# A hybrid layer's norms: reciprocal square roots by a power on GpSimd in place of Newton steps on VectorE

## The chip, the cores and the metric

The kernel runs on one core of a Trainium2 chip. The metric is the device time of one launch, in microseconds (us). The engines are named as in the profile: PE is TensorE (PEld its weight loads), DVE is VectorE, ACT is ScalarE, POOL is GpSimd, and SP is the engine that issues the transfers.

## The reference

One layer over a sequence of 2048 tokens of width 1024, all in float32. The rows of x are normalized and projected to the inputs of three mixers: a gated delta rule (4 heads of 128), an mLSTM (4 heads of 64) and an S5 state-space mixer (256 channels). Their outputs are projected back and added to x. A feed-forward with a convolution over tokens (2816 channels) and a last norm of the rows follow. Cut to the lines that matter here:

```python
def rms_norm(x, w):                      # rows, three times
    return x * lax.rsqrt(jnp.mean(x * x, -1, keepdims=True) + EPS) * w
def head_rms_norm(x, w):                 # outputs of the delta rule and the mLSTM
    return x * lax.rsqrt(jnp.mean(x * x, -1, keepdims=True) + EPS) * w
def l2_norm(x):                          # q and k of the delta rule
    return x * lax.rsqrt(jnp.sum(x * x, -1, keepdims=True) + EPS)

h = rms_norm(x, norm1_w);  proj = h @ w_in
q = l2_norm(silu(conv(q))) * GDN_DK ** -0.5;  k = l2_norm(silu(conv(k)))
y_a = head_rms_norm(gated_delta_rule_chunked(q, k, v, g, beta), norm_w) * silu(z)
y_b = sigmoid(o) * head_rms_norm(mlstm_chunked(...), norm_w)
x = x + concat(y_a, y_b, y_c) @ w_out
x = x + conv_ffn(rms_norm(x, norm2_w), ...)
return rms_norm(x, final_norm_w)
```

## The kernel before, in words

The sequence is worked through in four blocks of 512 tokens (NB = 4, BT = 512, four chunks of P = 128 tokens each). For each block a main stream of products (`main_a`) projects the normalized rows, one column tile of 128 after the other, and side streams do everything else: the delta rule of a head (`gdn`, 16 times), the mLSTM of a block (`mlstm`, four times), the S5 mixer, the preparation of the next block's rows (`x_prep`), and the rounding of weights. Then follow the output projection with the second norm (`out_proj`), the feed-forward in two halves of 1024 tokens (`ffn`), and the last norm (`final_sums`, `finals`).

Products in float32 are made of three in a shorter type: each weight tile is split into a rounded part and a rest (`split`). ACT writes the rounded part (`wh`, in the feed-forward `f_wh`), and POOL subtracts it from the tile (`wl`, `f_wl`), 1024 columns at a time. So POOL's queue holds mostly splits, and each waits for ACT.

The order in which instructions are emitted is not written out. Streams are Python generators; `drive` steps the one whose needs are met first by an estimate that the kernel itself keeps (`Clock`): it charges each instruction a cost by engine and size as it is emitted. What stands between two `yield`s of a stream is emitted in one go. Every engine then executes its instructions in the order of emission, and semaphores hold one that needs another engine's result.

The reciprocal square root is a helper, `rsqrt(y, x, t)`, on DVE alone: a guess from the bits of the float (a shift, then a multiplication and an addition of integers), and three Newton steps of three instructions. It has four callers, and each makes an affine step (scale the sum, add EPS) on DVE before it:

- `inv_rms`: norms of rows, from two half sums (tiles `rs`, `n_rs`, `f_rs`, one column for each row tile). ACT takes the squares and their sums.
- `gdn`, norms of q and k: eight columns, `s_ssq` to `s_rs`. The next instructions on DVE make `s_c` and `s_b` of the result, and from them the matrix `g_D` that POOL masks into `g_T`.
- `gdn`, the head norm: four columns, `s_so` to `s_ro`. DVE multiplies it by q's norm, scales the head's output with it into `gq`, and PE transposes that (`sd_py`).
- `mlstm`: 16 columns, all four chunks at once, after POOL has squared and DVE summed each chunk. It scales the output `mv`.

`s_t` is the temporary of the Newton steps in `gdn`. Nearly all instructions carry the line of the recording helper, L167, so groups are told apart by their tiles.

Of the kernel before, what the change touches and what calls it, by code (L numbers as in the profile page):

```python
# [7 lines left out]
F32 = mybir.dt.float32  # L8
F32R = mybir.dt.float32r
I32 = mybir.dt.int32  # L10
AF = mybir.ActivationFunctionType
ALU = mybir.AluOpType
# [3 lines left out]
DRAM = bass.MemoryType.DRAM  # L16

P = 128
L = 2048
DM = 1024  # L20
# [3 lines left out]
NCB = BT // P  # L24
# [4 lines left out]
EPS = 1e-6  # L29
# [4 lines left out]
# order of a block's heads (0-3), their gates (a-d) and the mLSTM's columns (m)  # L34
# [10 lines left out]
class Clock:  # L45
    """An estimate of when each engine reaches what was emitted for it, to order the emission by."""
# [35 lines left out]
    def span(self, ap):  # L82
        """Tile and the ranges of its elements of a partition"""
        if ap.space != SB:
            return ap.tensor.name, self.ALL
        dims = sorted((s, n) for s, n in ap.ap[1:] if n > 1 and s)
        size = 1
        while dims and (dims[0][0] <= size or len(dims) > 1 or dims[0][1] > 4):
            s, n = dims.pop(0)
            size += (n - 1) * s  # L90
        lo = ap.offset % ap.ap[0][0]
        s, n = dims[0] if dims else (0, 1)
        return ap.tensor.name, tuple((lo + i * s, lo + i * s + size) for i in range(n))

    def after(self, log, span, own, other):
        """Ends of what log has on a span: plus own[engine], or other"""
        name, rs = span
        t = 0.0
        for k, (end, by) in log.get(name, {}).items():
            if any(a < hi and lo < b for a, b in k for lo, hi in rs):  # L100
                t = max(t, end + own.get(by, other))
        return t

    def note(self, e, op, args, kw):
# [3 lines left out]
        # engines take turns at a bank  # L108
# [78 lines left out]
class Hybrid:  # L187
# [21 lines left out]
    def rsqrt(self, y, x, t):  # L209
        V = self.V  # L210
        V.tensor_scalar(out=y.bitcast(I32), in0=x.bitcast(I32), scalar1=1, scalar2=None,
                        op0=ALU.logical_shift_right)
        V.tensor_scalar(out=y.bitcast(I32), in0=y.bitcast(I32), scalar1=-1, scalar2=0x5F3759DF,
                        op0=ALU.mult, op1=ALU.add)
        for _ in range(3):
            V.tensor_tensor(out=t, in0=y, in1=y, op=ALU.mult)
            V.scalar_tensor_tensor(out=t, in0=t, scalar=-0.5, in1=x, op0=ALU.mult, op1=ALU.mult)
            V.scalar_tensor_tensor(out=y, in0=t, scalar=1.5, in1=y, op0=ALU.add, op1=ALU.mult)
# [15 lines left out]
    def setup(self):  # L234
        nc, ins, V, A, S = self.nc, self.ins, self.V, self.A, self.S
        cp = self.const = self.pool("const")
        self.dram = self.pool("dram", space=DRAM)
        self.pctx = ExitStack()
        self.ps = self.pool("ps", space=PSUM, ctx=self.pctx)
        self.ident = cp.tile([P, P], F32, name="ident")  # L240
        S.dma_start(out=self.ident, in_=self.cst_d[C_ID])

# [157 lines left out]
    def square_sums(self, xt, ss, junk):  # L400
        """ss[:, 0:2] = sums of the squares of the rows' halves"""
        for j in range(2):
            self.A.activation(out=junk, in_=xt[:, j * 512:(j + 1) * 512], func=AF.Square, accum_out=ss[:, j:j + 1])

    def inv_rms(self, out, ss, t):
        """out = 1 / rms of rows from ss (rows, n, 2)"""
        V = self.V
        V.tensor_tensor(out=t, in0=ss[:, :, 0], in1=ss[:, :, 1], op=ALU.add)
        V.tensor_scalar(out=t, in0=t, scalar1=1.0 / DM, scalar2=EPS, op0=ALU.mult, op1=ALU.add)
        self.rsqrt(out, t, ss[:, :, 0])  # L410
# [34 lines left out]
    def to_channels(self, xs, k, wcol, hi, lo, psum):  # L445
        """Channel block k of four row tiles, transposed, times the norm weight, in two parts."""
        ps = self.ps.tile([P, 4, P], F32, tag=psum[0], bufs=psum[1], name="psx")
        for j, x in enumerate(xs):
            self.T.transpose(out=ps[:, j, :], in_=x[:, k * P:(k + 1) * P], identity=self.ident)
        flat = ps.rearrange("p a b -> p (a b)")  # L450
        self.A.activation(out=hi, in_=flat, func=AF.Copy, scale=wcol)
        self.V.scalar_tensor_tensor(out=lo, in0=flat, scalar=wcol, in1=f32(hi), op0=ALU.mult, op1=ALU.subtract)

    def norm1(self, b, n, ps, w):
        """A block's normalized rows, transposed, with the products of its first column tile"""
# [23 lines left out]
    # what follows a column tile's products; tiles are followed in their order  # L479
# [72 lines left out]
    def ops_a(b):  # L552
        """Column tiles of a block: kind, index, first column of w_in."""
# [37 lines left out]
    def decay(self):  # L591
        """na = -exp(gdn_a_log)"""
# [6 lines left out]
    def gates(self, b, gs, gt):  # L599
# [18 lines left out]
        # log(1 + e) = 2 atanh(e / (2 + e))  # L618
# [9 lines left out]
        # q = log1p(e); softplus = max(y, 0) + q  # L628
        V.scalar_tensor_tensor(out=q, in0=y, scalar=0.0, in1=q, op0=ALU.max, op1=ALU.add)
        # beta = 1 / (1 + exp(y)) through e = exp(-|y|): (y < 0 ? 1 : e) / (1 + e)  # L630
# [9 lines left out]
        # g (h, c) and log f (c, h)  # L640
# [43 lines left out]
    def gdn(self, b, h, tiles, gz, gt):  # L684
        V, A, G, T, S = self.V, self.A, self.G, self.T, self.S
        n = b * H + h
# [19 lines left out]
        # transposes to token layout, with the sums of squares of k and q  # L706
# [36 lines left out]
        V.tensor_scalar(out=ssq, in0=ssq, scalar1=EPS, scalar2=None, op0=ALU.add)  # L743
        rs, t = sm("rs", 2 * NCB), sm("t", 2 * NCB)
        self.rsqrt(rs, ssq, t)
# [31 lines left out]
        # inverse of I + M by doubling of the diagonal blocks: Ti, and its transpose Vi beside it;  # L777
        # a level changes only the columns of Vi in the upper halves, those of Ti in the lower ones
# [44 lines left out]
        # the recurrence over chunks; the new values take the place of the old, the states that of the keys  # L823
# [28 lines left out]
        # head norm, gate  # L852
        so, t4 = sm("so"), sm("t4")
# [5 lines left out]
        V.tensor_scalar(out=so, in0=so, scalar1=1.0 / P, scalar2=EPS, op0=ALU.mult, op1=ALU.add)  # L859
        ro = sm("ro")  # L860
        self.rsqrt(ro, so, t4)
# [14 lines left out]
    def mlstm(self, b, kT, vT, og, gt):  # L876
# [13 lines left out]
        for c in range(NCB):  # L890
# [72 lines left out]
            # the chunk's results take the place of its values  # L963
# [8 lines left out]
        s2, s3 = tl("s2", [P, 16]), tl("s3", [P, 16])  # L972
        V.tensor_scalar(out=s1, in0=s1, scalar1=1.0 / 64, scalar2=EPS, op0=ALU.mult, op1=ALU.add)
        self.rsqrt(s2, s1, s3)
# [19 lines left out]
    def s5_setup(self, pool):  # L994
# [53 lines left out]
        # th = n pi/2 + r  # L1048
# [19 lines left out]
        # quadrant m in {-2..2}: odd: (m cos, -m sin); even: (s sin, s cos) with s = 1 - m^2 / 2  # L1068
# [58 lines left out]
        for q0 in range(0, NG, NQ):  # L1127
# [15 lines left out]
            for g0 in range(0, NQ, 4):  # L1143
# [8 lines left out]
                # the injections take the place of what was transposed  # L1152
# [9 lines left out]
        # rotor of one chunk and its modulus  # L1162
# [12 lines left out]
        # powers 0..15 of the rotor, and of its 16th power  # L1175
# [28 lines left out]
    def s5_first(self):  # L1204
        """The matrices of S5, in the place of the first block's rows"""
# [7 lines left out]
    def s5_run(self, ep, n0, N, QG):  # L1213
        """Chunks n0 .. n0 + N of the sequence, QG groups at a time; starts from self.s5c and leaves it for more."""
# [22 lines left out]
        for g0 in range(0, 16, QG):  # L1237
# [3 lines left out]
            # rotor powers 16 i + j from those of i and j  # L1241
# [15 lines left out]
            # injections, turned back  # L1257
# [82 lines left out]
    def w_out_load(self, wo, st):  # L1340
        """The two parts of w_out"""
# [20 lines left out]
    def out_prod(self, xs, y):  # L1362
        """The output projection of a tile of tokens, added to the first of xs"""
# [28 lines left out]
    def ffn_pools(self):  # L1392
        """Room for what follows the mixers, in their place"""
# [12 lines left out]
    def out_proj(self):  # L1406
        """Output projection, a tile of tokens after the other. While the last block is mixed there is room for
        the projection only, and the norm of such tiles comes later."""
# [74 lines left out]
    def norm2(self, i, x, r):  # L1483
        """A tile's rows, normalized and transposed: in two parts for the first half, to memory for the second"""
# [18 lines left out]
    class Weights:  # L1503
        """Weight tiles of the feed-forward in their order of use, loaded and split ahead."""
# [35 lines left out]
    def ffn_plan(self):  # L1540
        self.groups = [[m, m + 1] for m in range(0, MF, 2)]
        NH = L // HALF
        # the down products of a group come after the first up products of the next one
# [207 lines left out]
    def drive(self, main=None, cond=lambda: True):  # L1751
        """Steps main to its end, or without one the sides while cond holds."""
# [74 lines left out]
def _constants():  # L1827
# [8 lines left out]
    # level i: row s in the lower half of a block of 2w, column j the j-th of the columns in upper halves  # L1836
# [30 lines left out]
```

## Time and profile before

| | |
|---|---|
| time, median of 3 runs | 3026.31 us |
| the three runs | 3022.46, 3026.86, 3026.31 us |
| the profiled execution: its span, first to last instruction (the only time it is listed with) | 3025.7 us |
| PE, busy | 2798.8 us (93%) |
| DVE, busy | 2037.8 us (67%) |
| ACT, busy | 1142.8 us (38%) |
| POOL, busy | 837.1 us (28%), 536 instructions |
| mixers, until about | 1410 us |
| feed-forward, until about | 2996 us |

How to read the lines of the profile: a group's row has the engine, the operation, the tile written and the tiles read, the shapes, the count, the busy time with the mean duration in ns, and the idle time of that engine just before with what ended it. In a row of the timeline the first two numbers are the start in us from the span's start and the duration; x2 or x3 merges several alike; square brackets hold the idle time before and what ended it. A row of the waits has who waited for whom, the sum in us, how often, and the longest.

### The profile page before, as it was taken

Reading aid. Unit: us, or ns where it says so; the run is one execution under the profiler, and the core shown is the slowest. Engines: PE = TensorE matmul, PEld = TensorE weight load, DVE = VectorE, ACT = ScalarE, POOL = GpSimd, SP = SyncE. Lnnn points to the kernel's source line nnn. Section 1 sums busy time; section 2 is a strip of 40 time slices with the busy share of each in tenths; the row PEclk is TensorE's granted clock in tenths of the full one; section 3 lists DMA queues with packets and bytes.
Section 4 is the critical chain, followed back from the end, with each engine's and each line's share of the span. In section 5 each row is a group of like instructions: output and inputs, shape, how many; then the busy total and the mean of one; then the engine's idle time right before and its main releaser. Section 6 shows DMA issues by size and latency. Waiting matters only on the chain.

```text
span 3025.7 us, 37726 instructions
## 1 busy us (share of the span) xinstructions
PE 2798.8 (93%) x13826; PEld 2333.7 (77%) x13826; DVE 2037.8 (67%) x4524; ACT 1142.8 (38%) x2141; POOL 837.1 (28%) x536
## 2 busy tenths in 40 slices
PE   7887888978898888889999999999999999999997
PEld 5676777867787777678888888888888888888885
DVE  6877778688877886764446665666568665656566
ACT  4334444444454353533333333223344322333333
POOL 3253024222322342222322222222222222222223
PEclk9888899999999999979999999999999999999998
DMA  4222222223221322334561111111125111111111
GB/s 126 62 81 71 77 77 76 70 63 98 68 76 50 89 82 83 114 95 145 157 210 56 42 56 43 49 42 56 49 91 174 42 49 49 49 49 49 49 43 62
DMA packets 314944, 232.39 MB, mean 77 GB/s; under 512 B 36291, under 2 KB 286278, under 8 KB 314758
## 3 DMA queue, kind: packets, MB, share of 16 engines
q1 hardware_dynamic: 314758, 229.98, 25.3%
q8 instruction: 109, 1.79, 0.2%
q14 instruction: 77, 0.63, 0.1%
HBM read 192.06 MB, written 37.88 MB: 76 GB/s over the span
## 4 chain that ended last, share of the span: by engine, by line
PE 58%; DVE 7%; ACT 1%; issue 1%; DMA 0%; POOL 0%; ACTq 0%; SPq 0%; DVEq 0%; POOLq 0%
PE psf L167 32%; PE psd L167 16%; PE pso L167 5%; DVE acc L167 2%; PE sd_p L167 1%; PE sd_pw L167 1%; DVE s_t L167 1%; PE psx L167 0%; DVE e_x L167 0%; ACT junk L167 0%; PE psmo L167 0%; PE psq L167 0%; DVE g_D L167 0%; DVE f_rs L167 0%; PE sq L167 0%
## 5 line engine op out<-in xcount | busy, mean ns | idle before, releaser
L167 POOL TENSOR_TENSOR f_wl<-f_wr,f_wh 128x1024 fp32r<-128x1024 f32 x132 | 342.2, 2593 | 1073.0 <-ACT f_wh L167 1030.4
L167 PE MATMUL psf<-h2h,f_wh 128*128 128x512 f32 x1408 | 547.9, 389 | 0.0
L167 PE MATMUL psf<-h2h,f_wl 128*128 128x512 f32 x1408 | 547.9, 389 | 0.0
L167 PE MATMUL psf<-h2l,f_wh 128*128 128x512 f32 x1408 | 547.7, 389 | 0.0
L167 POOL TENSOR_TENSOR wl<-wr,wh 128x1024 fp32r<-128x1024 f32 x108 | 266.5, 2470 | 537.9 <-ACT wh L167 506.3
L167 DVE SCALAR_TENSOR_TENSOR f_cv<-f_raw,fpar,f_cv 128x512 f32<-128x512 f32 x352 | 264.2, 750 | 77.3 <-ACT f_cv L167 70.9
L167 ACT ACTIVATE f_raw<-psf 128x512 f32<-128x512 f32 x176 | 105.3, 598 | 539.0 <-issue 302.6
L167 DVE TENSOR_TENSOR f_acc<-f_acc,psd 128x512 f32<-128x512 f32 x352 | 229.2, 685 | 116.6 <-PE psd L167 113.9
L167 PEld LDWEIGHTS psf<-h2h,f_wl 128*128 128x128 f32 x1408 | 264.4, 188 | 54.8
L167 PEld LDWEIGHTS psf<-h2h,f_wh 128*128 128x128 f32 x1408 | 264.4, 188 | 54.8
L167 PEld LDWEIGHTS psf<-h2l,f_wh 128*128 128x128 f32 x1408 | 264.4, 188 | 54.7
L167 PE MATMUL psd<-f_wh,f_mh 128*128 128x512 f32 x704 | 278.1, 395 | 0.0
L167 PE MATMUL psd<-f_wl,f_mh 128*128 128x512 f32 x704 | 278.1, 395 | 0.0
L167 PE MATMUL psd<-f_wh,f_ml 128*128 128x512 f32 x704 | 277.9, 395 | 0.0
L167 DVE COPY f_halo<-f_raw 128x2 f32<-128x2 f32 x176 | 73.3, 416 | 278.1 <-ACT f_raw L167 276.9
L167 ACT ACTIVATE f_wh<-f_wr 128x1024 fp32r<-128x1024 f32 x132 | 139.3, 1056 | 269.2 <-issue 263.6
L167 DVE COPY f_raw<-f_halo 128x2 f32<-128x2 f32 x176 | 203.9, 1158 | 0.0
L167 DVE SCALAR_TENSOR_TENSOR acc<-raw,par,acc 128x512 f32<-128x512 f32 x192 | 183.7, 957 | 4.6
L167 PEld LDWEIGHTS psd<-f_wh,f_ml 128*128 128x128 f32 x704 | 132.0, 187 | 32.3
L167 PEld LDWEIGHTS psd<-f_wl,f_mh 128*128 128x128 f32 x704 | 132.0, 187 | 32.3
L167 PEld LDWEIGHTS psd<-f_wh,f_mh 128*128 128x128 f32 x704 | 132.0, 187 | 32.2
L167 ACT ACTIVATE f_cv<-psf,fpar 128x512 f32<-128x512 f32 x176 | 136.6, 776 | 0.0
(486 smaller groups left out, 5599.0 us busy)
## 6 DMA issues: line engine op xcount, KB each, us to landing
wr<-in_w_in_dram SPq DMA_DIRECT2D x104, 512.0 KB
f_wr<-in_w_up_dram SPq DMA_DIRECT2D x88, 512.0 KB
f_wr<-in_w_down_dram SPq DMA_DIRECT2D x44, 512.0 KB
xt<-in_x_dram SPq DMA_DIRECT2D x16, 512.0 KB
y<-y_d SPq DMA_DIRECT2D x16, 512.0 KB
f_acc<-x_d SPq DMA_DIRECT2D x16, 512.0 KB
o_x<-in_x_dram SPq DMA_DIRECT2D x12, 512.0 KB
x_d<-o_x SPq DMA_DIRECT2D x12, 512.0 KB
```

The lines of the kernel that those rows point to most:

```text
L167: return f(*args, **kw)
```

## The change

`rsqrt(y, x, a, s)` now computes (s x + a) to the power of -1/2. It takes the affine step over from its callers, as one instruction on DVE, and has POOL raise the result to the power held in a constant tile, `mhalf`, which a memset on DVE fills at the start. The bit guess, the Newton steps and their temporaries are gone. The rest of the diff removes comments.

```diff
-    def rsqrt(self, y, x, t):
-        V = self.V
-        V.tensor_scalar(out=y.bitcast(I32), in0=x.bitcast(I32), scalar1=1, scalar2=None,
-                        op0=ALU.logical_shift_right)
-        V.tensor_scalar(out=y.bitcast(I32), in0=y.bitcast(I32), scalar1=-1, scalar2=0x5F3759DF,
-                        op0=ALU.mult, op1=ALU.add)
-        for _ in range(3):
-            V.tensor_tensor(out=t, in0=y, in1=y, op=ALU.mult)
-            V.scalar_tensor_tensor(out=t, in0=t, scalar=-0.5, in1=x, op0=ALU.mult, op1=ALU.mult)
-            V.scalar_tensor_tensor(out=y, in0=t, scalar=1.5, in1=y, op0=ALU.add, op1=ALU.mult)
+    def rsqrt(self, y, x, a, s):
+        self.V.tensor_scalar(out=y, in0=x, scalar1=s, scalar2=a, op0=ALU.mult, op1=ALU.add)
+        self.G.tensor_tensor(out=y, in0=y, in1=self.mhalf[:, 0:y.shape[1]], op=ALU.pow)
...
     def setup(self):
...
+        self.mhalf = cp.tile([P, 16], F32, name="mhalf")
+        V.memset(self.mhalf, -0.5)
...
     def inv_rms(self, out, ss, t):
         V.tensor_tensor(out=t, in0=ss[:, :, 0], in1=ss[:, :, 1], op=ALU.add)
-        V.tensor_scalar(out=t, in0=t, scalar1=1.0 / DM, scalar2=EPS, op0=ALU.mult, op1=ALU.add)
-        self.rsqrt(out, t, ss[:, :, 0])
+        self.rsqrt(out, t, EPS, 1.0 / DM)
...
     def gdn(self, b, h, tiles, gz, gt):
...
-        V.tensor_scalar(out=ssq, in0=ssq, scalar1=EPS, scalar2=None, op0=ALU.add)
-        rs, t = sm("rs", 2 * NCB), sm("t", 2 * NCB)
-        self.rsqrt(rs, ssq, t)
+        rs = sm("rs", 2 * NCB)
+        self.rsqrt(rs, ssq, EPS, 1.0)
...
-        V.tensor_scalar(out=so, in0=so, scalar1=1.0 / P, scalar2=EPS, op0=ALU.mult, op1=ALU.add)
         ro = sm("ro")
-        self.rsqrt(ro, so, t4)
+        self.rsqrt(ro, so, EPS, 1.0 / P)
...
     def mlstm(self, b, kT, vT, og, gt):
...
-        s2, s3 = tl("s2", [P, 16]), tl("s3", [P, 16])
-        V.tensor_scalar(out=s1, in0=s1, scalar1=1.0 / 64, scalar2=EPS, op0=ALU.mult, op1=ALU.add)
-        self.rsqrt(s2, s1, s3)
+        s2 = tl("s2", [P, 16])
+        self.rsqrt(s2, s1, EPS, 1.0 / 64)
```

More of the change, by code (lines that the diff above doesn't have):

```diff
@@ L851, in gdn @@
         self.misc.append(self.cur)
-        so, t4 = sm("so"), sm("t4")
+        so = sm("so")
         junk = mkj()
```

## The prediction

> **What bounds the kernel now.** I began with the page's slices of TensorE (PE), in tenths of each fortieth of the span.
>
> ```profile
> PE   7887888978898888889999999999999999999997
> ```
>
> PE is full from about the twentieth slice to the last but one, and at seven to nine tenths before. I cut the span where that changes.
>
> ```profile
> core 0: us, PE busy (x) PEld busy (x) DVE busy (x) ACT busy (x) POOL busy (x), PEclk, DMA share, GB/s
> 0.00:1410.00 1410.00, 1204.77 (x6796) 1025.45 (x6797) 1061.31 (x2978) 597.15 (x1309) 424.44 (x367) 0.93 0.29 83
> 1410.00:1560.00 150.00, 148.60 (x714) 123.52 (x713) 64.29 (x210) 56.91 (x92) 51.29 (x29) 1.00 0.53 166
> 1560.00:2996.00 1436.00, 1436.00 (x6280) 1177.42 (x6280) 891.51 (x1288) 476.27 (x716) 349.53 (x137) 1.00 0.19 60
> 2996.00:3026.00 30.00, 9.44 (x41) 7.26 (x39) 20.72 (x50) 12.42 (x24) 11.83 (x5) 0.74 0.35 140
> ```
>
> The columns are the stretch, its length, and each engine's busy time with its instructions. In the output projection and the feed-forward (1410 to 2996) PE is idle 1.4 us of 1586: what VectorE (DVE) saves there is hidden behind the products, and if that cover went, DVE would still have 40% of idle time. In the mixers' stage (0 to 1410) PE idles 205 us and DVE 349 us: neither is full, so dependences decide. The last 30 us hold hardly any products. Next come the waits of the first stage, and the chain that ended last over 990 to 1410 us (it is not followed further back).
>
> ```profile
> PE sd_py L167 <- DVE gq L167: 26.5, 7, 6.5
> ...
> PE sd_v L167 <- DVE g_D L167: 8.9, 4, 3.3
> ```
>
> ```profile
> by line: DVE acc L167 11.3%; PE pso L167 9.8%; PE sd_p L167 4.9%; PE sd_pw L167 4.5%; DVE s_t L167 4.5%; issue 3.2%; DVE e_x L167 3.0%; ACT junk L167 2.8%; PE psmo L167 2.7%; PE psq L167 2.7%; DVE g_D L167 2.5%; PE sq L167 2.3%; PE sd_o L16
> ```
>
> gq is what the head norm scales, so PE stands 26.5 us in 7 waits right behind that norm, and 8.9 us in 4 behind g_D, which needs the norms of q and k. s_t, the temporary of the Newton steps, holds 4.5% of the 420 us of chain, 18.9 us. So the stage does pay for this arithmetic, in places.
>
> **The change, part by part.** The program takes 60 of these roots: 32 in the delta rule, 4 in the mLSTM, 24 over rows (6 into rs, 12 into n_rs, 6 into f_rs). Each loses 2 integer and 9 Newton instructions on DVE, keeps its affine step, and gains one power on GpSimd (POOL) with a hop there and one back. A quiet root, on DVE:
>
> ```profile
> 123.98 0.16 DVE L167 TENSOR_SCALAR s_ssq<-s_ssq 128x8 f32<-128x8 f32 x1
> ...
> 126.39 0.16 DVE L167 TENSOR_TENSOR s_c<-Gbeta,s_rs 128x4 f32<-128x4 f32 x1
> ```
>
> From the affine step's end (124.14) to s_c, which needs the result (126.39), pass 2.25 us. For the hops the trace has a round trip of the same kind, the squares that POOL takes between two DVE instructions of the mLSTM:
>
> ```profile
> L167 POOL TENSOR_TENSOR m_wk<-mv x16: 612/612/613, 346.0 to 1350.2; 128x256 f32<-128x256 f32 x16
> ...
>   POOL m_wk L167: 12.9, 16
> ```
>
> DVE idled 12.9 us in 16 such trips, 0.81 us each, of which the square itself is 0.61: the two hops are 0.19 us. With a power of p the root now takes 0.19 + p, and saves 2.06 - p.
>
> No power is in the trace. POOL's rows bound it:
>
> ```profile
> L167 POOL TENSOR_TENSOR wl<-wr,wh 128x1024 fp32r<-128x1024 f32 x108 | 266.5, 2470 | 537.9 <-ACT wh L167 506.3 <-PE psz L167 16.9 <-DVE e_Cr L167 14.7
> ...
> L167 POOL TENSOR_TENSOR t_x<-t_BB,t_Ai 128x64 f32<-128x64 f32 x32 | 11.5, 358 | 0.0
> ```
>
> From 64 elements in 0.36 us and 1024 in 2.47 the fixed part is 0.22 us, so p for 1 to 16 elements is hardly below 0.23 us. Above, I bound it by a whole weight split, 2.47 us. In size it is nearest the short row, but a power is more than one multiplication, so I take the geometric middle, 0.75 us. That saves 1.31 us a root; the ends give 1.83 and -0.41. In the delta rule and the mLSTM the next DVE instruction needs the result, so all that is queued on DVE stands still for 0.94 us; that is within these numbers. On rows, ACT (ScalarE) waits for the result and DVE goes on.
>
> The old steps have another cost, where POOL splits a weight meanwhile:
>
> ```profile
> 1137.39 2.34 POOL L167 TENSOR_TENSOR wl<-wr,wh 128x1024 fp32r<-128x1024 f32 x1 [4.30 <-ACT wh L167]
> ...
> 1137.50 2.24 DVE L167 SCALAR_TENSOR_TENSOR s_t<-s_t,s_so 128x4 f32<-128x4 f32 x1
> ...
> 1140.99 1.11 PE L167 MATMUL sd_py<-ident,gq 128*128 128x128 f32 x4 [6.49 <-DVE gq L167]
> ```
>
> ```profile
> 0.00:1410.00 1410.00, 67.44 (x288) 0.93 0.29 83
> ```
>
> A step of 0.16 us took 2.24 and ended with the split, and PE waited 6.49 us. The 288 Newton steps of the delta rule (second row) would be 47.2 us at the 0.166 and 0.162 us of the quiet ones, but took 67.44: 20.2 us of such stalls, some ten. [...]
>
> In the instance above the stalled step is the eighth of nine, some 1.6 us in, when a power of 0.75 us would be over and the result used. A stall stays where the split comes within p: I keep a third of them (0.75 of 2.1 us) and count 13.5 us as gone.
>
> Is POOL free when the power comes? A split reaches POOL after ACT has rounded its weight. The squares, which ACT also takes, stand in one uninterrupted step with the root of the head norm, so a split that ACT rounds later is queued behind the power. It is otherwise where another stream's step comes between:
>
> ```profile
> 850.69 0.16 DVE L167 TENSOR_TENSOR s_c<-Gbeta,s_rs 128x4 f32<-128x4 f32 x1
> ...
> 851.62 2.41 POOL L167 TENSOR_TENSOR wl<-wr,wh 128x1024 fp32r<-128x1024 f32 x1 [7.60 <-ACT wh L167]
> ...
> 853.99 1.30 POOL L167 TENSOR_TENSOR g_T<-g_D,cst 128x512 f32<-128x512 f32 x1
> ```
>
> g_T is emitted in the same step as this root and yet follows the split: the split was queued first. The power would start at 854.03 and s_c at 854.97 instead of 850.69, 4.3 us later. By the timeline three of the 36 roots stand so (the others near 993 and 1293 us): 13 us lost.
>
> Sum for DVE in the mixers' stage: 33 x 1.31 = 43, and 13.5 of stalls, less 13: 44 us of 1061 busy. How much reaches the end? The 11 waits of PE above can lose at most 11 x 1.31 = 14 us, and the stalls in them (six of the ten, 8 us): 22 us. A PE that is fed sooner runs into its next wait. If over half is given back, 10 us stay. I take 16, the middle.
>
> Tail. The three last roots (f_rs, of 4, 2 and 2 columns) lie on the chain; on DVE, the second and third:
>
> ```profile
> 3005.73 2.63 DVE L167 TENSOR_SCALAR f_rs<-f_rs 128x2 f32<-128x2 f32 x3
> ...
> 3010.03 1.88 DVE L167 TENSOR_TENSOR f_acc<-f_acc,psd 128x512 f32<-128x512 f32 x3
> 3011.82 2.43 DVE L167 TENSOR_SCALAR f_acc<-f_acc,f_rs 128x512 f32<-128x512 f32 x1
> 3014.18 2.29 DVE L167 TENSOR_TENSOR f_rs<-f_ss 128x2 f32<-128x2 f32 x1
> ...
> 3018.76 1.27 DVE L167 TENSOR_SCALAR f_acc<-f_acc,f_rs 128x512 f32<-128x512 f32 x3
> ```
>
> Before each, a step is held by POOL's scaling of the same rows (2.63 us for three steps; 2.29 for one), and that stays, since the power is queued behind that scaling anyway. After it, ACT's next scaling waits for 0.94 us instead of about 2.1, and DVE adds the last products meanwhile. Each root brings about 1.15 us: 3.4 us for three.
>
> Start. The first two roots precede the first products, but ACT, which must scale, is still summing squares under the first. I set their gain to nothing; it is at most 2 x 1.31. [...]
>
> Edits at nothing: a memset of 16 columns while DVE waits for the first rows of x; the temporary's place in memory; less DVE work under the feed-forward. The emission order follows the kernel's own estimate of each engine, which now charges DVE 11 instructions less a root and POOL one more, so streams swap places. No row prices that; I allow PE's longest wait in the row above, 6.5 us, either way.
>
> Total: 16 + 3.4 = 19.4 us. The profiled execution's span is 3025.7 us, 0.6 below the median of 3026.31. 3026.3 - 19.4 = 3007 us.
>
> **The rivals.**
> (a) The power is dear, and DVE's wait for it costs more than the steps did: slower. With the share that I let through (16 of 44) each microsecond of p costs 36 x 0.36 = 13 us in the mixers and 3 in the tail; at p = 2.06 only the stalls' 5 us are left, so it turns at p = 2.4, the duration of a split. At p = 4 it is 1.94 x 16 - 5 = 26 us: 3052. For it: nothing in the trace excludes it, and POOL is the slower engine on equal work. Against: 2 to 16 columns. Chance 0.17.
> (b) The queue: the new order puts powers behind splits that wait for ACT. One more such place costs 4.3 + 1.31 = 5.6 us of DVE, of which 2 us come through, so ten more, 13 of 36, take the whole gain: 3026. For it: the split above had kept POOL's queue waiting for ACT for 7.60 us. Against: the one-step argument. Chance 0.07.
> (c) Hidden: the mixers give all of it back, PE being at 85% there, and only the tail stays: 3023, within the noise. Against: the chain's 18.9 us of s_t. Chance 0.11.
> (d) More than forecast: the chain rules, on which nine tenths of the s_t steps of its 420 us lie. 0.9 x 44 + 3.4 = 43 us: 2983. Chance 0.10.
>
> **How the numbers follow.** The forecast has 0.55, with a range of its own of 2993 to 3020 (10 to 22 us from the mixers, 3 from the tail, 6.5 for the order). About 6 us, 0.2%, is what a measurement can tell from no change. Faster: 0.55 + 0.10 = 0.65. Same: 0.07 + 0.11 = 0.18. Slower: 0.17. The range takes in the better half of (a), to 3036, and the nearer part of (d), from 2988.
>
> **What would show it.** Right: powers of 8 columns of 0.5 to 1.0 us that start within 0.2 us of the affine step; some 44 us less of DVE's time from the affine steps to their users before 1410 us; PE's waits for gq down by a third to a half; the same length from the output projection to the last product; the end shorter by 3 us. Wrong: powers above 2 us; s_c and s_ro waiting for POOL by several microseconds, with a split ahead of the power; new stalls of 2 us in s_c, s_b or s_ro; or a lighter DVE and an unchanged end of the mixers.

## The result, and the profile after

The changed kernel takes 3048.26 us, the median of four runs (3046.66 to 3053.9); the kernel before took 3025.26, by four runs too. The ratio is 1.0084, with a 95% interval of 1.007 to 1.0098: 23 us slower, where 19 us faster was forecast. The profiled execution after has a span of 3045.7 us.

The page's slices of PE after, as the prediction shows them of before:

```profile
PE   7887788988998889879999999999999999999998
```

They differ from those of before by a tenth here and there and do not show the loss. I cut the trace of both kernels at the first product of the feed-forward (`psf`). The first fence is of the kernel before, the second of the changed one, from 19 us (the first projection) to that cut; the columns are those of the prediction's table.

```profile
19.00:1554.00 1535.00, 1343.67 (x7470) 1141.39 (x7469) 1111.09 (x3136) 639.90 (x1375) 465.65 (x388) 0.93 0.31 90
```

```profile
19.00:1578.80 1559.80, 1355.94 (x7471) 1152.61 (x7470) 1002.09 (x2577) 644.25 (x1378) 529.14 (x440) 0.93 0.30 88
```

DVE is busy 109 us less (1111 to 1002) in 559 fewer instructions, and yet this stretch is 24.8 us longer. That is the whole loss and a little more: from the first `psf` to the last product both kernels take about 1452 us, and after the last product the changed one takes 14.5 us instead of 20.2. The 24.8 us are PE's: it idles 203.9 us instead of 191.3, and the same 7470 products take 1355.9 us instead of 1343.7. The loss arises in the first three blocks: the main stream's first product of the fourth comes 29.6 us later (961.9 to 991.5 us), and from there to the first `psf` the changed kernel is 4.8 us shorter.

Did the power do it? POOL's groups of the changed kernel say what one costs:

```profile
L167 POOL TENSOR_TENSOR s_rs<-s_rs,mhalf 128x8 f32<-128x8 f32 x16 | 26.3, 1643 | 92.8 <-DVE s_rs L167 92.7
...
L167 POOL TENSOR_TENSOR s_ro<-s_ro,mhalf 128x4 f32<-128x4 f32 x16 | 16.2, 1013 | 111.0 <-DVE s_ro L167 108.8 <-PE psmv L167 2.2
...
L167 POOL TENSOR_TENSOR m_s<-m_s,mhalf 128x16 f32<-128x16 f32 x4 | 11.6, 2907 | 11.1 <-DVE m_s L167 10.0 <-PE sq L167 1.0
...
L167 POOL TENSOR_TENSOR n_rs<-n_rs,mhalf 128x1 f32<-128x1 f32 x13 | 7.1, 544 | 41.5 <-DVE n_rs L167 41.5
...
L167 POOL TENSOR_TENSOR rs<-rs,mhalf 128x2 f32<-128x2 f32 x2 | 1.4, 704 | 9.0 <-DVE rs L167 9.0
```

That is near 0.39 us and 0.157 for each column. For the 4, 8 and 16 columns of the delta rule and the mLSTM it is dearer than the 0.75 that I took, for 8 columns twice as dear; for 1 and 2 columns it is cheaper. (The new order takes one more root over rows, 13 instead of 12 into `n_rs`.) But DVE waits for it for less time than the Newton steps had held it. The waits of the changed kernel from 19 to 1600 us:

```profile
DVE s_c L167 <- POOL s_rs L167: 31.5, 16, 4.6
...
PE sd_py L167 <- DVE gq L167: 18.5, 8, 8.1
...
DVE s_ro L167 <- POOL s_ro L167: 18.0, 16, 1.1
...
PE sd_gk L167 <- DVE g_kdec L167: 15.3, 3, 8.8
...
DVE mv L167 <- POOL m_s L167: 12.1, 4, 3.0
```

The sixteen waits each for q's and k's norms (the user is `s_c`) and for the head norm (the user is `s_ro`), and four for the mLSTM's, come to 31.5 + 18.0 + 12.1 = 61.6 us. Before, DVE spent 103.6 us from the affine step's end to the same users in the same 36 places (read off the timeline, stalls behind splits included). And PE's waits right behind the head norm fell from 26.5 us to 18.5. So the roots became cheaper, as forecast, and the kernel slower. What grew are waits with no root in them, such as PE for `g_kdec`: 15.3 us in three, where the kernel before had this:

```profile
PE sd_gk L167 <- DVE g_kdec L167: 3.4, 1, 3.4
```

`g_kdec` is k scaled by a decay, before it is normed. One of the three, in the timeline of the changed kernel:

```profile
980.84 1.06 ACT L167 ACTIVATE wh<-wr 128x1024 fp32r<-128x1024 f32 x1
...
981.65 3.21 DVE L167 SCALAR_TENSOR_TENSOR g_D<-g_E,Ggc,cst 128x128 f32<-128x128 f32 x4
...
981.97 2.48 POOL L167 TENSOR_TENSOR wl<-wr,wh 128x1024 fp32r<-128x1024 f32 x1 [8.27 <-ACT wh L167]
...
987.27 0.69 DVE L167 TENSOR_TENSOR g_kdec<-sd_k,s_e 128x512 f32<-128x512 f32 x1 [2.34 <-ACT junk L167]
...
988.02 2.08 PE L167 MATMUL sd_gk<-gk 128*128 128x128 f32 x8 [8.85 <-DVE g_kdec L167]
...
988.93 0.17 DVE L167 TENSOR_SCALAR s_rs<-s_ssq 128x8 f32<-128x8 f32 x1
```

PE stands 8.85 us. Ahead of that, ACT rounds a weight for the main stream at 980.84, DVE's four steps of `g_D` take 3.21 us while the split of it runs on POOL (the four steps of `g_DT` at 987.88, of the same shape, take 1.13), and the chain runs on over ACT's `junk` sums to `g_kdec`. The root of this head starts at 988.93, after the wait is over. So something other than the root's own time has changed. I took it to be the order, that is, which stream's work stands where; the experiments test that.

### The profile page after: what moved, and what is told of

Its sections match the earlier page's. It is cut to its first block, busy times and chain, and to the rows that moved or that the text cites. A ratio compares the mean times of both kernels' runs of the same rounds, so it can differ in the third digit from the quotient of the medians.

```text
span 3045.7 us, 37155 instructions
## 1 busy us (share of the span) xinstructions
PE 2812.0 (92%) x13826; PEld 2345.2 (77%) x13826; DVE 1911.7 (63%) x3867; ACT 1146.0 (38%) x2144; POOL 906.1 (30%) x597
## 4 chain that ended last, share of the span: by engine, by line
PE 56%; DVE 3%; issue 1%; ACT 1%; POOL 1%; DMA 0%; POOLq 0%; ACTq 0%; SPq 0%; DVEq 0%
PE psf L167 31%; PE psd L167 16%; PE pso L167 5%; DVE acc L167 1%; PE sd_p L167 1%; PE sd_pw L167 1%; PE psx L167 0%; PE psv L167 0%; PE psq L167 0%; PE psk L167 0%; DVE e_x L167 0%; PE sd_pt L167 0%; DVE e_yo L167 0%; PE pi L167 0%; PE sq L167 0%
## 5 line engine op out<-in xcount | busy, mean ns | idle before, releaser
L167 DVE COPY f_raw<-f_halo 128x2 f32<-128x2 f32 x176 | 197.6, 1123 | 0.0
L167 PEld LDWEIGHTS psd<-f_wh,f_ml 128*128 128x128 f32 x704 | 132.2, 188 | 31.5
```

Of the source, the lines that this page charges most:

```text
L167: return f(*args, **kw)
```

## The experiments

Two theories. **Order:** the kernel's estimate charges DVE and POOL differently now, so `drive` emits the streams in another order, and that order is worse; the power itself gains. **Power** (rival (a)): a power of 1 to 2.9 us, with DVE standing still, costs more than it saves, and the order is a side matter.

**The old order with the power.** The estimate is charged the eleven old steps; the chip runs the power. By the traces PE, ACT and SP get exactly the sequence of instructions of the kernel before.

```diff
 def rsqrt(self, y, x, t):          # of the kernel before
-    V.tensor_scalar(...)           # and the ten other steps
+    f = lambda op, **kw: self.clock.note("V", op, (), kw)
+    f("tensor_scalar", out=y.bitcast(I32), in0=x.bitcast(I32))   # and the ten others: charged, not emitted
...
+    self.G.eng.tensor_tensor(out=y, in0=x, in1=self.mhalf[:, 0:y.shape[1]], op=ALU.pow)
...
+        V.eng.memset(self.mhalf, -0.5)               # in setup, not charged
```

> The roots are computed as in the changed kernel (affine step on DVE, power on POOL), but the kernel's own estimate is charged the old integer and Newton steps, so every engine gets its instructions in the order of the kernel before. Theory A (the loss of 0.8% is the new emission order; the power itself is a gain of 0.5 to 1.1 us a root): faster than before by 8 to 20 us, about 3005 to 3018 us. Rival B (the power and DVE's in-order wait for it cost the time, whatever the order): 3040 to 3052 us, as the changed kernel. Rival C (root work is hidden in the mixers, the order does nothing either): 3020 to 3026 us.

Measured: 2997.03 us, ratio 0.9901 (0.9888 to 0.9914). The power alone gains 28.7 us.

**The new order with Newton steps.** The mirror image, on the changed kernel.

```diff
 def rsqrt(self, y, x, a, s):       # of the changed kernel
+    self.clock.note("V", "tensor_scalar", ...)    # the affine step: charged
+    self.clock.note("G", "tensor_tensor", ...)    # the power: charged, not emitted
+    V.tensor_scalar(out=x, in0=x, scalar1=s, scalar2=a, ...)     # emitted, then the eleven old steps
-    self.G.tensor_tensor(..., op=ALU.pow)
```

> The counterpart: the estimate is charged the affine step and the power, so the order is that of the changed kernel, but the chip runs the old integer and Newton steps on DVE. Theory A: slower than the changed kernel, since it has the bad order and the dearer roots: 3050 to 3070 us. Rival B: about the time of the kernel before, 3020 to 3030 us. Rival C: 3040 to 3050 us.

Measured: 3086.22 us, ratio 1.0198 (1.0184 to 1.0212). The order alone, with no power at all, costs 60.5 us; put under the same order, the power gains 38.0. The order theory stands and the other falls. The stretch from 19 us to the first `psf`, first for the old order with the power, then for the new order with Newton steps:

```profile
19.00:1527.40 1508.40, 1336.95 (x7472) 1137.95 (x7471) 1011.41 (x2575) 638.08 (x1375) 530.10 (x439) 0.94 0.32 91
```

```profile
19.00:1610.30 1591.30, 1372.21 (x7473) 1162.48 (x7471) 1107.59 (x3149) 644.23 (x1378) 464.09 (x388) 0.92 0.30 86
```

With the two fences of the result these are the four corners: 1508 and 1535 us at the old order, 1560 and 1591 at the new. The products are the same in all four. Of ACT's 6 us between 638 and 644, three more of its ACT_TABLE_LOADs make 3.8 (73 for 70, of 1.28 us each); for the rest it is places that differ. The wait of 8.85 us above is there too without a power; its row in the timeline of the new order with Newton steps:

```profile
1010.01 2.07 PE L167 MATMUL sd_gk<-gk 128*128 128x128 f32 x8 [8.85 <-DVE g_kdec L167]
```

**Telling the estimate the true price.** The estimate charges a power like any POOL step, 0.17 us for 8 columns. Here it is told the measured price.

```diff
         if e == "G":
+            if kw.get("op") == ALU.pow:
+                return 0.39 + 0.157 * n
             return n / 476 + 0.15
```

> The changed kernel, with the estimate charging a power what its rows measured: 0.39 us and 0.157 us a column (544 ns for 1, 1013 for 4, 1643 for 8, 2907 for 16), where it had 0.15 us and 0.002 us a column. A third emission order with the same arithmetic. Theory A with an order that can be mended by a truer price: 3005 to 3025 us. Theory A with orders that fall by chance: anywhere from 3005 to 3060 us. Rival B: 3040 to 3052 us, as the price of the power is the same.

Measured: 3023.76 us, ratio 0.9996 (0.9983 to 1.0008). A third order, 24.5 us better than the changed kernel's and 26.7 worse than the old one with the power. So a truer price does not bring the old order's place back. This order has 80 table loads, more than the slower changed kernel, so these do not explain the loss. It also differs from the changed kernel in nothing but the order, where the corners of old and new order differ as well in the temporaries that they allocate.

**Is the new order bad, or the old one good?** Three kernels that change nothing but a constant of the estimate in the kernel before, by 0.01 or less, and so run Newton steps in other orders. `SEM` is what the estimate charges for a semaphore; 0.07 is the fixed part of a DVE instruction.

```diff
-    SEM = 0.26
+    SEM = 0.27        # in one kernel; 0.25 in another
...
-            return n / 960 + (0.13 if op == "scalar_tensor_tensor" and n > 64 else 0.07)
+            return n / 960 + (0.13 if op == "scalar_tensor_tensor" and n > 64 else 0.072)    # in the third
```

> The kernel before, its arithmetic untouched; only the estimate's charge for a semaphore goes from 0.26 to 0.27 us, which changes the emission order. It measures how far order alone moves the time. Theory A: a shift of the size of the change's own, 10 to 30 us either way, is possible. Rivals B and C: within 6 us of 3025.

> The kernel before with its arithmetic untouched; the estimate's fixed charge for a DVE instruction goes from 0.07 to 0.072 us. A second sample of how far order alone moves the time. If the order of before is an unusually good one among its neighbours: slower by 10 to 60 us, 3035 to 3085. If orders scatter around it: as often faster as slower, 2990 to 3060.

> The kernel before with the semaphore charge at 0.25 us instead of 0.26: a third neighbour of its order, Newton steps untouched. If the order of before is unusually good among its neighbours (0.27 gave 3075.0, the other charge 3065.0): 3035 to 3085 us. If orders scatter about it: as likely below 3025.

Measured: 3075.0 us (ratio 1.0165, 1.0151 to 1.018) with 0.27; 3064.99 (1.0125, 1.011 to 1.0141) with 0.072; 3042.8 (1.0064, 1.0052 to 1.0076) with 0.25. With the new order's 3086.2 all four neighbours of the old order are slower, by 18.1 to 60.5 us. The old order is the best of the five tried, and the change lost that place; why it is a good one, no run shows.

**The power at two of these orders.** The edit of the first experiment, with `SEM` at 0.27 and at 0.25.

> The order of the kernel with the semaphore charge of 0.27 us (3075.0 us with Newton steps), computed with the power: the estimate is charged the old steps. Theory A (order and arithmetic add up; at two orders the power brought 28.7 and 38 us): 3037 to 3048 us. Rival D (the gain of the power belongs to the old order, where its waits happened to stand in PE's way): anywhere from 3025 to 3080 us.

> The order of the run before this one (semaphore charge 0.25 us), computed with the power, the estimate charged the old steps. A fourth pair of arithmetics at one order, after gains of 28.7, 38 and 13.6 us: 10 to 40 us faster than that run. If the power loses at any order, that it gains always falls.

Measured: 3061.4 us (ratio to the kernel before 1.0111, 1.0093 to 1.0128), 13.6 less than Newton steps at that order, where 27 to 38 were expected; and 3012.47 (0.9956, 0.9944 to 0.9968), 30.3 less. The four pairs, with DVE's time from affine step to user in the 36 places, read off the timelines:

| order | median, Newton to power | DVE in the 36 roots | first `psf` at |
|---|---|---|---|
| before's | 3025.7 to 2997.0: -28.7 | 103.6 to 68.2: -35.4 | 1554.0 to 1527.4: -26.6 |
| `SEM` 0.25 | 3042.8 to 3012.5: -30.3 | 94.5 to 59.1: -35.4 | 1572.5 to 1546.9: -25.6 |
| the change's | 3086.2 to 3048.3: -38.0 | 96.6 to 61.6: -35.0 | 1610.3 to 1578.8: -31.5 |
| `SEM` 0.27 | 3075.0 to 3061.4: -13.6 | 93.0 to 66.8: -26.2 | 1601.5 to 1592.1: -9.4 |

The power gains at every order. At 0.27 it saves DVE less, since Newton steps had cost less there and two powers stood behind a split (6.92 and 3.62 us to the user), and only a third of the saving comes through. The stretch to the first `psf`, first with Newton steps, then with the power:

```profile
19.00:1601.50 1582.50, 1374.10 (x7472) 1170.01 (x7470) 1104.70 (x3149) 643.66 (x1380) 465.88 (x388) 0.91 0.30 86
```

```profile
19.00:1592.10 1573.10, 1381.50 (x7474) 1175.27 (x7472) 998.76 (x2577) 644.85 (x1380) 532.96 (x440) 0.91 0.31 87
```

PE's idle time falls by 16.8 us (208.4 to 191.6), much as in the other three pairs (14.0 to 19.8). But the same products take 7.4 us more, where in the other three they take 6.7 to 16.3 us less. Why they do so at this order stays open.

**What a microsecond of root costs.** At the old order: the power twice (the second with exponent 1, which leaves the value as it is), and a product of the same shape in the power's place, which leaves the reciprocal root out.

```diff
+        self.G.eng.tensor_tensor(out=y, in0=y, in1=self.one16[:, 0:y.shape[1]], op=ALU.pow)   # twice
...
-        self.G.eng.tensor_tensor(..., op=ALU.pow)
+        self.G.eng.tensor_tensor(..., op=ALU.mult)                                            # product
```

> The old order with the power, and behind each power a second one on POOL, with exponent 1, so that a root costs 1.64 (8 columns), 1.01 (4), 2.91 (16) us more. In the mixers that is 16 x 1.64 + 16 x 1.01 + 4 x 2.91 = 54 us more of DVE's waiting. If the share that reaches the end is that of the first test (26.6 us before the feed-forward for about 47 us of DVE time saved, 0.57): 31 us and 2 to 3 in the tail, 3030 us. If the price of the power is hidden: 2997 to 3003 us. If DVE's waits reach the end whole: 3053 us.

> The old order, with a product by 0.01 on POOL where the power was: the reciprocal root is left out, the instruction, its queue and both hops are kept. It shows what the power's own price of 0.54 to 2.91 us costs. A product of 1 to 16 columns should take about 0.25 us, so the 36 roots lose 16 x 1.4 + 16 x 0.75 + 4 x 2.65 = 45 us of DVE's waiting and the tail 2 us. If the share that reaches the end is that of the first test, 0.57: 2970 us. If it is 1, as the doubled power had it: 2952 us. If the hops and the queue were the cost and not the power: 2990 to 2997 us.

Measured: 3054.43 us (1.0093, 1.0079 to 1.0106) and 2943.76 (0.9731, 0.9718 to 0.9744), 57.4 above and 53.3 below the single power. The waits of each kernel from 19 to 1600 us, first the power twice, then the product:

```profile
DVE s_c L167 <- POOL s_rs L219: 64.4, 16, 8.9
...
DVE s_ro L167 <- POOL s_ro L219: 36.5, 16, 2.3
...
DVE mv L167 <- POOL m_s L219: 24.0, 4, 6.0
```

```profile
DVE s_c L167 <- POOL s_rs L218: 13.9, 16, 5.8
...
DVE s_ro L167 <- POOL s_ro L218: 6.4, 16, 0.7
...
DVE mv L167 <- POOL m_s L218: 1.3, 4, 0.3
```

Their sums are 124.9 and 21.6 us, against 68.2 with one power: 56.7 more and 46.6 less. The first `psf` came 52.8 us later and 52.2 earlier. So at this order a microsecond in which DVE stands for a root is about a microsecond at the end (0.93 and 1.12 of it). Rival (a) can be read off the same three times: on the line from one power to two, the time of the kernel before is reached at one and a half powers.

**Where the rows' roots matter.** The power at the old order, but Newton steps in `inv_rms`.

```diff
     def inv_rms(self, out, ss, t):
-        self.rsqrt(out, t, ss[:, :, 0])
+        self.newton(out, t, ss[:, :, 0])     # the eleven old steps
```

> The old order, with the power in the delta rule and the mLSTM only; the 24 roots over rows keep their Newton steps on DVE. If the mixers' gain comes from the 36 roots that DVE waits for, and the rows matter in the tail alone (15.5 us behind the last product with the power, 20.3 before): 3001 to 3004 us. If the rows' roots free DVE in the mixers too: 3005 to 3015 us.

Measured: 3002.55 us, ratio 0.9924 (0.9911 to 0.9937). The first `psf` is at 1527.6 us, as with powers (1527.4); after the last product it takes 20.2 us, not 15.5. All that the 24 roots over rows bring, they bring in the tail.

**A wait only for what is needed.** The next DVE instruction after q's and k's root needs k's four columns alone. At the old order the power of 8 is cut in two of 4, k's first.

```diff
+        n = y.shape[1]
+        for k in (0, 4) if n == 8 else (0,):
+            m = 4 if n == 8 else n
-        self.G.eng.tensor_tensor(out=y, in0=x, in1=self.mhalf[:, 0:n], op=ALU.pow)
+            self.G.eng.tensor_tensor(out=y[:, k:k + m], in0=x[:, k:k + m], in1=self.mhalf[:, 0:m], op=ALU.pow)
```

> The old order with the power; the power of the norms of q and k (8 columns) is split into two of 4, k's first. The next DVE steps (s_c, s_b, g_D) need k's norm alone, so DVE should wait for 1.0 us instead of 1.64, while q's power runs behind. If DVE waits for the first power only: 16 x 0.63 = 10 us less waiting, at a share of 0.6 to 1 that reaches the end, 2987 to 2992 us. [...]

Measured: 2988.03 us, ratio 0.9875 (0.9862 to 0.9888): 9.0 us below the single power, as expected, and faster than both kernels of the case. Two rows of the waits from 19 to 1600 us, of the single power at the old order and of the split one:

```profile
DVE s_c L167 <- POOL s_rs L218: 36.9, 16, 7.2
```

```profile
DVE s_c L167 <- POOL s_rs L221: 26.8, 16, 6.6
```

DVE waits 10.1 us less, and the first `psf` comes 9.3 us earlier.

## Why the prediction was wrong

**The step that failed is the emission order.** The text saw that "streams swap places", set it at nothing and allowed 6.5 us either way, by the longest wait of PE. That is the size of one wait, and an order moves all of them at once. Measured, the change's order costs 51.2 us with powers (2997.0 to 3048.3) and 60.5 with Newton steps; the five orders with Newton steps spread over 60.5 us. The change is the power's -28.7 us and the order's +51.2, together 22.5 of the 23 us measured. No rival had the order as its mechanism: (b) only let it put powers behind splits, and the changed kernel has one such among its 32 delta-rule roots (4.59 us to the user, for 1.75 in a quiet place).

**What the order does** is seen in part. Between the old and the new order, both with powers, the stretch before the first `psf` grows by 51.4 us, of which 32.4 are PE's idle time (171.5 to 203.9) and 19.0 are the same products taking longer. Around the wait of 8.85 us the changed kernel shows longer products behind a wait:

```profile
968.00:979.00 11.00, 6.37 (x34) 4.59 (x33) 8.67 (x25) 3.55 (x6) 2.49 (x2) 1.00 0.50 135
979.00:988.00 9.00, 0.17 (x2) 0.00 (x0) 4.68 (x8) 7.04 (x20) 2.48 (x1) 0.55 0.26 70
988.00:992.00 4.00, 3.98 (x17) 3.91 (x18) 2.11 (x10) 2.78 (x9) 1.64 (x1) 0.50 0.10 39
992.00:1003.00 11.00, 10.65 (x77) 9.65 (x76) 9.47 (x24) 3.20 (x5) 2.89 (x3) 0.93 0.00 0
```

The granted clock is full (1.00) up to 979 us, 0.55 on average over the 9 us in which the wait lies, and half (0.50) over the 17 products of the 4 us that follow it. The product of `hh` and `wh` into `psg` (128x512) that starts at 991.46 us takes 0.78 us, the next one, at 996.36, 0.47. The rows show wait, lower clock and longer products one after the other; that the first brings the others is my reading. Over the four corners and the kernel with `SEM` at 0.27 the busy time of these products rises from 1337 to 1374 us as the granted clock falls from 0.94 to 0.91. The idle time in all does not settle it: with `SEM` at 0.27 and the power PE idles 191.6 us, as in the kernel before (191.3), yet the products take 1381.5 us instead of 1343.7. Which swaps of the order open such waits is not settled: no run here moved single streams.

**The power's price was too low, and the share that reaches the end too.** DVE was to save 44 us and 16 of them were to come through, a share of 0.36. At the old order it saved 35.4 from the affine steps to their users. Of that the quiet price gave 21.5 us where 43 were set, since 8 columns take 1.64 us and not 0.75 (in equal work POOL is the slower engine, as rival (a) had it: in the kernel before a product of 128x512 takes 1.41 us on POOL, `gq` by `g_E`, and 0.68 on DVE, `sd_v` by `s_c`); the rest are stalls, of which more were gone by then than was set. Of the 35.4, 26.6 us came through, a share of 0.75 (the expectations' 0.57 took 47 us for the saving, which is too much). The argument that a PE fed sooner runs into its next wait was wrong at this order: the three experiments that changed only what POOL does for a root, and with it DVE's wait by 10 to 57 us, brought 0.92 to 1.12 of that to the first `psf`. With `SEM` at 0.27 the share was 0.36, so no one share holds for all orders. The price and the share were wrong in opposite ways and offset each other in part, by luck; the mixers' gain of 26.6 us at the old order lies above the forecast's 10 to 22, on the side of rival (d).

**Stalls and the queue.** In the kernel before, the 36 roots took 22.9 us more than 36 quiet ones (103.6, for 16 of 2.25, 16 of 2.21 and four of 2.34 us). At the old order with the power they took 9.0 us more, of which 8.7 are two powers behind a split (5.02 and 7.20 us to the user, for 1.76). So the queue took 8.7 us where 13 were set for three, and 0.3 us is all that is left for stalls up to the user. But stalls came back at the user itself (new ones of 2 us in `s_ro` were among the prediction's signs of a wrong forecast): at the old order a split right behind the power holds four of the 16 products by q's norm and three of the eight steps of `mv`, and these users take 13.6 us more than in the kernel before. Of the 22.9 us of stalls 9.3 are gone, not the two thirds that the forecast set by estimate. The timeline of the changed kernel has such a place at 289 us:

```profile
288.13 1.02 POOL L167 TENSOR_TENSOR s_ro<-s_ro,mhalf 128x4 f32<-128x4 f32 x1 [10.08 <-DVE s_ro L167]
...
289.12 2.34 POOL L167 TENSOR_TENSOR wl<-wr,wh 128x1024 fp32r<-128x1024 f32 x1
289.18 2.30 DVE L167 TENSOR_TENSOR s_ro<-s_ro,s_rs 128x4 f32<-128x4 f32 x1 [1.13 <-POOL s_ro L167]
```

The multiplication of `s_ro` by q's norm starts 0.06 us after the split and ends with it, 2.30 us later; `s_c`, of the same shape, takes 0.16 us.

**Right:** PE's waits for `gq`, which were to fall by a third to a half, fell from 26.5 to 6.9 us at the old order (18.5 at the new); the feed-forward did not move (1451 to 1454 us in all); the tail gained 4.7 us at the old order and 5.7 in the changed kernel, for 3.4 forecast, and POOL's scaling still held the affine steps (2.2 to 2.3 us, where a quiet one takes 0.17), as said. In quiet places of the changed kernel the hops were 0.08 us from DVE to POOL and 0.03 back, 0.11 for the 0.19 taken. The rows' roots brought nothing ahead of the tail. At the start, whose gain was set at nothing, the changed kernel's first power begins at 8.33 us, 0.08 us after its affine step, and takes 0.71 us; the second, of the same shape, takes 0.70.

## What to carry to other kernels

Where a kernel orders its own instructions by an estimate, a cheaper operation is two changes, and the reordering can be the larger: measure the operation with the old charges kept, and a few neighbouring orders beside it, before judging either. Price a moved wait by the columns that it waits for, and split it so that the next instruction waits only for what it reads. And where dependences decide, and neither engine is full, do not set the share that reaches the end at a third without a measurement: here it was 0.36 to 0.90 from Newton steps to the power, by order, and 0.92 to 1.12 where only POOL's part of the root changed.

## What was not expected of the hardware

A power on POOL costs by the column: 0.54 us for one column of 128 partitions, 1.64 for 8, 2.91 for 16, where a product of 4, 8 or 16 columns in the same places of the delta rule and the mLSTM took 0.20 to 0.22 us. And the same products cost more in some orders than in others: 7470 of them took 1337 to 1382 us, with a granted clock of 0.94 to 0.91, and 38 us lie between two kernels in which PE idles about 191 us alike.
